# Quarter sums of the down projection's operands formed by DRAM transfers instead of DVE, in a fp32 decoder layer

## Chip, cores and metric

One core of a Trainium2 chip. The metric is the device time of one execution in microseconds (us). The kernel before ran three times; the median counts.

## What is computed

One decoder layer on a sequence of 1024 tokens with 1024 features, all in float32. Only the lines that matter here:

```
n1 = rms_norm(h, g_mix);  proj = n1 @ w_in
y_conv = short_conv_mixer(...);  y_attn = native_sparse_attention(...)
h = h + concatenate([rms_norm(y_conv), rms_norm(y_attn)]) @ w_out
u = causal_dwconv(rms_norm(h, g_ffn) @ w_up, w_ffn_conv)
u_gate, u_val = split(u)
h = h + (silu(u_gate) * u_val) @ w_down          # D_FF = 2816
h = h + sigmoid(rms_norm(h, g_ple) @ w_ple_gate) * (p @ w_ple_proj)
return rms_norm(h, g_final)
```

The attention has three branches: compressed blocks, the best 8 selected blocks of 64 keys, and a window of 512.

## The kernel before

Float32 products are formed from parts: each operand x is split into hi (a rounded copy, made on ACT, line 101) and lo = x - hi (DVE, line 104), and `mm3` (lines 189 to 193) issues three matmuls, hi by hi, hi by lo and lo by hi. The order of work on each engine is set by the framework's scheduler, from a simulated timeline, within the dependencies; the order of transfers of one queue is set with it. SP's queue issues nearly all loads and stores, POOL's queue the accumulating transfers; each queue issues in order, so one transfer that waits for a free buffer holds all behind it.

The stages are: the input projections (to about 280 us), the attention in eight blocks of 128 queries in the order 3, 7, 6, 5, 4, 2, 1, 0 (to about 550 us), the out projection `out_half` (its weights are raw tiles `out_r`, split into `out_p`), the norm that gives the operands `m` of the up phase, the up phase (22 pairs j of a gate and a value column block, to about 1075 us), the down phase (to about 1295 us), the gate of the layer embedding and the final norm.

Up and down use a scheme of seven products for a 2x2 block multiplication instead of eight. The up phase takes for pair j the raw weights `ugr` and `uvr` (`up_weights`, line 1004), forms from their halves four sums on DVE (`ut` in two parts, `u7s`, `u3s`, lines 1018 to 1021), and splits all into parts. `up(j)` (line 1149) runs the seven products; ACT copies (`e`) and DVE additions drain them from PSUM, then come the convolution of three taps (lines 1179 to 1181), silu and a multiplication (line 1184) on DVE, and the result `uc` is stored to DRAM as `ad[j]` (line 1185).

The down phase goes through the products n in the order 1, 2, 6, 5, 7, 3, 4 with 11 steps each. Its weights `down_r` are 256 KB each; the sums that products 5, 6, 7 and 3 need are formed in DRAM (`wsum`) by eight POOL transfers in the attention stage (`down_weights`, line 922, one per block at line 955). The activations come back from `ad` as `ar` (line 1199, 22 loads of 512 KB), and the sums of their halves that the seven products need are formed on DVE (lines 1204 to 1216): 55 operations. Each operand is then split on ACT and DVE into `a`, and the products accumulate in PSUM (`da`, `db`, `d`); `res_add` adds or subtracts a finished product from the residual stream `hres`.

Beside these: in the attention, `factor` (line 584) makes on POOL the factors `sf` and others, `choose` (line 644) subtracts a maximum from `sc` on POOL and normalises it (lines 649 and 660), `finish` adds the block's output `ya` on POOL (line 825); the mask copies `mk` (line 716) are on POOL too. `attn_norm` (line 900) normalises `ya` into `yan` before the second half of the out projection.

## Time and profile before

| | us |
|---|---|
| three runs | 1409.8, 1407.91, 1410.55 |
| median | 1409.8 |
| the profiled execution | 1407.71 |
| its span in the trace | 1405.8 |

The profiled execution is 2.1 us below the median, and the span lies 1.9 us below its own time (work around the span). Sums are made against the profiled execution. PE in the profile is TensorE. A busy PE may still run at the lower clock; the views by stretches give the granted clock as a share of full speed (PEclk) and the number of matmuls started.

### The profile page before, as it was taken

What the parts mean: (1) busy time and instruction counts of PE and PEld (TensorE: products, weight loads), DVE (VectorE), ACT (ScalarE), POOL (GpSimd) and SP (SyncE); (2) the same over time, 40 slices, a digit from 0 to 9 for tenths busy, and PEclk for the clock granted to TensorE, in tenths of its full rate; (3) what the DMA queues carried; (4) which work ended last, traced back from release to release, by engine and by line L of the source; (5) the groups of instructions that cost most, each with busy time, mean ns of one, the idle gap of its engine ahead of it and who ended that gap; (6) DMA issues with size and microseconds to landing.
All of it is one profiled execution on the core that took longest, in us unless ns stands there. A gap on an engine that the chain in (4) does not pass through costs nothing.

```text
span 1405.8 us, 17553 instructions
## 1 busy us (share of the span) xinstructions
PE 1349.2 (96%) x6395; PEld 1061.7 (76%) x6395; DVE 990.3 (70%) x1803; ACT 643.0 (46%) x1095; POOL 141.7 (10%) x155
## 2 busy tenths in 40 slices
PE   8989999999999988899999999999997999999995
PEld 6879888865666666687888888888885788888884
DVE  7752332478777775798976887679878985667668
ACT  6232111177767652455543444345445434546433
POOL 0211001231222444000000000000000000000001
PEclk9999999999999999899999999999999899999998
DMA  7473211132635566741222222222257833322434
GB/s 271 114 182 120 97 46 45 30 97 76 113 113 113 165 165 176 234 169 51 90 75 84 76 80 87 78 73 93 75 178 250 327 94 94 98 75 60 152 104 179
DMA packets 78933, 168.82 MB, mean 120 GB/s; under 512 B 6912, under 2 KB 28416, under 8 KB 78848
## 3 DMA queue, kind: packets, MB, share of 16 engines
q1 hardware_dynamic: 69632, 141.49, 31.3%
q0 software_dynamic: 9216, 26.22, 7.6%
q8 instruction: 50, 0.82, 0.2%
q14 instruction: 35, 0.29, 0.1%
HBM read 133.08 MB, written 51.38 MB: 131 GB/s over the span
## 4 chain that ended last, share of the span: by engine, by line
PE 88%; DVE 6%; DMA 2%; SPq 1%; issue 1%; ACT 1%; POOL 0%; DVEq 0%; ACTq 0%; POOLq 0%
PE ua L193 4%; PE ua L191 4%; PE ua L192 4%; PE uc L191 3%; PE uc L193 3%; PE uc L192 3%; PE sy L770 2%; PE da L191 2%; PE d L193 2%; PE d L191 2%; PE d L192 2%; PE da L192 2%; PE wy L770 2%; PE da L193 2%; PE g L191 2%; PE g L192 2%
## 5 line engine op out<-in xcount | busy, mean ns | idle before, releaser
L1358 POOL DMA_DIRECT2D out_dram<-h x8 | 4.4, 555 | 826.1 <-DVE h L1357 826.1
L101 ACT ACTIVATE down_p<-down_r 128x512 fp32r<-128x512 f32 x77 | 47.8, 626 | 72.8 <-PE da L193 26.1
L104 DVE TENSOR_TENSOR down_p<-down_r,down_p 128x512 fp32r<-128x512 f32 x77 | 52.4, 687 | 29.3 <-ACT down_p L101 29.2
L1179 ACT ACTIVATE uc<-xg,vec 128x1024 f32<-128x1024 f32 x22 | 25.3, 1151 | 97.0 <-DVE xg L1172 97.0
L1172 DVE TENSOR_TENSOR xg<-uc,e 128x512 f32<-128x512 f32 x22 | 15.2, 691 | 74.3 <-PE uc L193 74.1
L101 ACT ACTIVATE in_h<-in_r 128x1024 fp32r<-128x1024 f32 (+1 forms) x20 | 20.7, 1037 | 96.6 <-PE cx L192 30.1
L191 PE MATMUL da<-a,down_p 128*128 128x512 f32 x132 | 54.2, 411 | 7.7 <-ACT down_p L101 7.7
L101 ACT ACTIVATE a<-ar 128x512 fp32r<-128x512 f32 x66 | 40.5, 624 | 35.1 <-PE d L193 16.0
L104 DVE TENSOR_TENSOR a<-ar,a 128x512 fp32r<-128x512 f32 x66 | 44.5, 686 | 14.7 <-ACT a L101 14.5
L722 ACT ACTIVATE ps<-ps,stat 128x512 f32<-128x512 f32 (+7 forms) x64 | 49.1, 770 | 12.4 <-DVE stat L733 12.1
L193 PE MATMUL da<-a,down_p 128*128 128x512 f32 x132 | 51.3, 404 | 3.1 <-DVE down_p L104 3.1
L192 PE MATMUL da<-a,down_p 128*128 128x512 f32 x132 | 54.2, 410 | 0.0
L193 PE MATMUL d<-a,down_p 128*128 128x512 f32 x132 | 52.1, 395 | 0.0
L191 PE MATMUL d<-a,down_p 128*128 128x512 f32 x132 | 52.1, 395 | 0.0
L192 PE MATMUL d<-a,down_p 128*128 128x512 f32 x132 | 52.0, 394 | 0.0
L104 DVE TENSOR_TENSOR in_l<-in_r,in_h 128x1024 fp32r<-128x1024 f32 (+2 forms) x22 | 25.0, 1141 | 28.3 <-ACT in_h L101 28.2
L191 PE MATMUL g<-g,pg_h 128*128 128x256 f32 (+1 forms) x128 | 43.5, 339 | 0.0
L192 PE MATMUL g<-g,pg_h 128*128 128x256 f32 (+1 forms) x128 | 43.2, 338 | 0.0
L193 PE MATMUL g<-g,pg_l 128*128 128x256 f32 (+1 forms) x128 | 43.1, 338 | 0.0
L641 ACT ACTIVATE pw<-pw,stat 128x640 f32<-128x640 f32 (+3 forms) x56 | 38.2, 685 | 6.0 <-DVE stat L695 3.2
L101 ACT ACTIVATE ugh<-ugr 128x1024 fp32r<-128x1024 f32 x22 | 23.4, 1061 | 37.4 <-DMA ugr<-in_w_up_dram 37.1
L101 ACT ACTIVATE uth<-ut 128x1024 fp32r<-128x1024 f32 x22 | 23.3, 1061 | 37.1 <-DVE ut L1019 37.1
(789 smaller groups left out, 4457.7 us busy)
## 6 DMA issues: line engine op xcount, KB each, us to landing
wsum<-in_w_down_dram POOLq DMA_DIRECT2D x6, 2816.0 KB, 18.8
uvr<-in_w_up_dram SPq DMA_DIRECT2D x22, 512.0 KB, 3.6
ugr<-in_w_up_dram SPq DMA_DIRECT2D x22, 512.0 KB, 4.4
ad<-uc SPq DMA_DIRECT2D x22, 512.0 KB, 2.6
ar<-ad SPq DMA_DIRECT2D x22, 512.0 KB, 5.9
down_r<-wsum SPq DMA_DIRECT2D x44, 256.0 KB, 2.6
in_r<-in_w_in_dram SPq DMA_DIRECT2D x18, 512.0 KB, 6.8
down_r<-in_w_down_dram SPq DMA_DIRECT2D x33, 256.0 KB, 4.4
```

The costliest lines, as they stand in the source:

```text
L101: nc.scalar.activation(hi, x, AF.Copy)
L104: (nc.gpsimd if (lo_eng or lo_of[0]) == "pool" else nc.vector).tensor_sub(lo, x, f32(hi))
L191: first = nc.tensor.matmul(ps, wh, mh, start=start, stop=False, **more)
L192: nc.tensor.matmul(ps, wh, ml, start=False, stop=False, **more)
L193: return first, nc.tensor.matmul(ps, wl, mh, start=False, stop=stop, **more)
L641: nc.scalar.activation(w[:, :b.nw * P], w[:, :b.nw * P], AF.Exp, bias=b.M_W[:, h:h + 1], scale=-1.0, accum_out=b.D_W[:, h:h + 1])
L722: nc.scalar.activation(w[:, :nk], w[:, :nk], AF.Exp, bias=b.M_S[:, h:h + 1], scale=-1.0, accum_out=b.D_S[:, h:h + 1])
L770: m = nc.tensor.matmul(py[64 * g:64 * g + 64, :], vals(n, g), pts[g], start=n == 0, stop=n == nblk - 1)
L1172: nc.vector.tensor_add(xg[:, hi], c, e2)
L1179: nc.scalar.activation(u, xe[:, 0:S], AF.Copy, scale=col(tap))
L1358: nc.gpsimd.dma_start(out[k], o)
```

## The change

Four things.

1. The sums of the activations that the down phase needs are formed by POOL transfers from DRAM to DRAM in the up phase (`act_sums`, called after each store of `ad[j]`): for j below 11 a copy of one half to three places (768 KB), a copy of the other half (256 KB) and an accumulating transfer of 768 KB, for j from 11 two accumulating transfers (768 and 256 KB), 55 in all. The signs that an addition can't give are put into what is stored: `ad[j]` is stored with one half negated, the weights of products 1 and 7 are negated in their split, and `res_add` takes other signs.
2. `operand` loads each of the 77 operands (256 KB) straight into its page and splits it in place; no `ar`, no sums on DVE. The first four go into pages of another size (`wpage`, in the profile "fp"), and each is issued behind an earlier weight load.
3. The weight sums of four pairs of the up phase (0, 1, 20, 21) are formed in DRAM (`usum`) as well, and `up_weights` loads them for these pairs. Together with the eight transfers of `wsum` these are 24, issued four a block in six blocks, two in the middle of the block (behind `factor`'s work) and two at its end.
4. The sides of two products change: `res_sq` of half 0 moves from product 5 to product 2, `res_split` from product 3 to product 6.

```diff
+    def split(x, hi, lo, hi_eng="act", lo_eng=None, minus=False):
+        if minus:
+            nc.scalar.activation(hi, x, AF.Copy, scale=-1.0)
+            nc.vector.scalar_tensor_tensor(lo, x, -1.0, f32(hi), op0=ALU.mult, op1=ALU.subtract)
+            return
...
-                split(raw, hi, lo)
+                split(raw, hi, lo, minus=key[:5] in ("down1", "down7"))
...
-        for do, dst, src in ((copy, w5, a[1][0]), (more, w5, a[1][1]), (copy, w6, w5), (more, w6, a[0][0]),
-                             (copy, w3, w6), (more, w3, a[0][1]), (copy, w7, a[1][0]), (more, w7, a[0][0])):
-            behind(do(dst, src), pooled[0])
-            yield
+        down_ = chain([[w_down[u * (NF // 2):(u + 1) * (NF // 2)][:, :, hs(q)].rearrange("j p n -> p j n") for u in range(2)]
+                       for q in range(2)], *(wsum[q].rearrange("j p n -> p j n") for q in range(4)))
+        up_ = []
+        for r, j in enumerate((0, NF - 2)):
+            a = [[w_up[2 * j + q:2 * j + q + 3:2][:, :, hs(u)].rearrange("j p n -> p j n") for u in range(2)] for q in range(2)]
+            dst = usum[2 * r:2 * r + 2].rearrange("j p n -> p j n")
+            up_.append(chain(a, *(dst[:, :, k * 512:k * 512 + 512] for k in (1, 0, 2, 3))))
+        for items in zip(down_, *up_):
+            for do, dst, src in items:
+                behind(do(dst, src), pooled[0])
+                yield
...
         merge((selected(cur), 9, 0, 1), (values(cur), min(i + 1, 5) + 3, 0, 1), (some(fill, more[0]), more[0], 0, 1))
+        for _ in range(2):
+            next(dsums, None)
...
         merge(*gens)
-        next(dsums)
+        for _ in range(2):
+            next(dsums, None)
...
-        nc.vector.tensor_add(t[:, two], v[:, one], v[:, two])
-        nc.vector.tensor_add(t[:, one], g[:, one], t[:, two])
-        nc.vector.tensor_add(a7, g[:, one], v[:, one])
-        nc.vector.tensor_add(a3, g[:, two], t[:, one])
+        if j in SUMMED:
+            src = usum[SUMMED[j]]
+            load(t, src[:, 0:S])
+            load(a7, src[:, S:S + 512])
+            load(a3, src[:, S + 512:])
+        else:
+            nc.vector.tensor_add(t[:, two], v[:, one], v[:, two])
...
-        nc.vector.tensor_mul(us[1], us[0], us[1])
+        plus, minus = (hs(0), hs(1)) if j < NF // 2 else (hs(1), hs(0))
+        nc.vector.tensor_mul(us[1][:, plus], us[0][:, plus], us[1][:, plus])
+        nc.vector.scalar_tensor_tensor(us[1][:, minus], us[0][:, minus], -1.0, us[1][:, minus], op0=ALU.mult, op1=ALU.mult)
         load(ad[j], us[1])
+        act_sums(j)
...
+    def act_sums(j):
+        a, d = ad[j], asum[j % NH_]
+        def three(half):
+            return a[:, half].unsqueeze(1).to_broadcast([P, 3, 512])
+        if j < NH_:
+            nc.gpsimd.dma_start(d[:, 0:3], three(one))
+            nc.gpsimd.dma_start(d[:, 3], a[:, two])
+            nc.gpsimd.dma_start(d[:, 0:3], three(two), accum_op=ALU.add)
+        else:
+            nc.gpsimd.dma_start(d[:, 1:4], three(two), accum_op=ALU.add)
+            nc.gpsimd.dma_start(d[:, 2], a[:, one], accum_op=ALU.add)
...
     def operand(n, j):
-        while len(raws) < min(NF, (j if n == 1 else j + NH_ if n == 2 else NF) + 5):
-            raws.append(page([P, S], f"ar{len(raws)}"))
-            load(raws[-1], ad[len(raws) - 1])
...
+        src = {1: ad[j][:, one], 2: ad[j + NH_][:, one], 3: ad[j + NH_][:, two],
+               5: asum[j][:, 0], 6: asum[j][:, 1], 4: asum[j][:, 2], 7: asum[j][:, 3]}[n]
+        t = (wpage if n == 1 and j < 4 else page)([P, 2, 512], f"a{n}_{j}", F32R)
+        hi, lo = t[:, 0], t[:, 1]
+        x = load(f32(lo), src)
+        if len(sent_w) > 3:
+            behind(x, sent_w[-3])
+        operands[n, j] = in_place(lo, hi)
...
     def begin_down():
-        prepare(3)
+        prepare(4)
```

The number of matmuls stays (6160 rows of PE in both programs). DVE has 1738 rows instead of 1787, ACT 938 instead of 939, POOL 203 instead of 136, SP 432 instead of 365.

How the order of the instructions moves at three places:

ACT, at the start of the second half of the out projection (`facc` is the sum of squares, `an0rr` the root of the attention norm, `yan` its operands, `out_p` the split weights). Before:

```order
L221 ACTIVATE facc_5084<-hx_4122 128x512
L233 ACT_TABLE_LOAD
L233 ACTIVATE an0rr<-an0s,eps 128x16
L224 ACTIVATE f11sq<-hx_4386 128x512
L101 ACTIVATE yan_5148<-ya_2052 128x512
L101 ACTIVATE yan_5152<-ya_2053 128x512
L101 ACTIVATE yan_5156<-ya_2054 128x512
L101 ACTIVATE out_p<-out_r 128x512 x2
```

Now:

```order
L227 ACTIVATE facc_5102<-hx_4139 128x512
L105 ACTIVATE out_p<-out_r 128x512 x2
L239 ACT_TABLE_LOAD
L239 ACTIVATE an0rr<-an0s,eps 128x16
L230 ACTIVATE f11sq<-hx_4405 128x512
L105 ACTIVATE out_p<-out_r 128x512
L105 ACTIVATE yan_5166<-ya_2054 128x512
```

The two weight tiles are split ahead of the norm's root, no longer behind three of its four results; DVE's order follows.

SP's queue, at the turn from up to down, from the sixth of the `ar` loads that stand together. Before:

```order
L1199 DMA ar_8916<-ad 128x1024
L1199 DMA ar_8922<-ad 128x1024
L155 DMA down_6_r<-in_w_down_dram 128x512
L1199 DMA ar_8948<-ad 128x1024
L1199 DMA ar_8971<-ad 128x1024
L1185 DMA ad<-uc_8670 128x1024
L155 DMA down_1_r<-in_w_down_dram 128x512
```

Now, from the first weights of the down phase on:

```order
L159 DMA down_0_r<-in_w_down_dram 128x512
L159 DMA down_3_r<-in_w_down_dram 128x512
L159 DMA down_1_r<-in_w_down_dram 128x512
L1248 DMA a_4_9034<-ad 128x512
L159 DMA down_6_r<-in_w_down_dram 128x512
L1215 DMA ad<-uc_8752 128x1024
L1248 DMA a_0_8990<-ad 128x512
L1248 DMA a_1_8994<-ad 128x512
L1248 DMA a_2_8998<-ad 128x512
L159 DMA down_2_r<-in_w_down_dram 128x512
```

Three weight loads come ahead of all operands but none of the 512 KB loads is left; of the operands, a_1 (and a_3, further on) wait for matmuls that read their pages.

POOL, in the first attention block of the loop (`sf`, `sc`, `pc`, `wf` are the work of `factor` and `choose`, `ya` the output of the block). Before:

```order
L589 TENSOR_TENSOR sf_2194<-stat_1726,gates 128x4x64 x2
L649 TENSOR_TENSOR sc_2197<-sc_2197,stat_2061 128x512
L660 TENSOR_TENSOR sc_2197<-sc_2197,stat_2061 128x512
L683 TENSOR_TENSOR pc_2364<-sc_2197,gates 128x4x64 x2
L589 TENSOR_TENSOR wf_2369<-stat_2061,gates 128x4x64 x2
L825 TENSOR_TENSOR ya_2052<-ws_2186,ss_2377 128x128
```

Now:

```order
L600 TENSOR_TENSOR sf_2196<-stat_1728,gates 128x4x64 x2
L948 DMA wsum<-in_w_down_dram 128x11x512
L948 DMA usum<-in_w_up_dram 128x2x512
L660 TENSOR_TENSOR sc_2201<-sc_2201,stat_2063 128x512
L671 TENSOR_TENSOR sc_2201<-sc_2201,stat_2063 128x512
L694 TENSOR_TENSOR pc_2368<-sc_2201,gates 128x4x64 x2
```

Two transfers stand between `sf` and `sc` where there was none; the other two of a block follow the four `ya`.

## Rows read from the trace of the kernel before

**Rows 1.** The page: span, busy time by engine, and the chain's shares.

```profile
span 1405.8 us, 17553 instructions
...
PE 1349.2 (96%) x6395; PEld 1061.7 (76%) x6395; DVE 990.3 (70%) x1803; ACT 643.0 (46%) x1095; POOL 141.7 (10%) x155
...
PE 88%; DVE 6%; DMA 2%; SPq 1%; issue 1%; ACT 1%; POOL 0%; DVEq 0%; ACTq 0%; POOLq 0%
```

**Rows 2.** Stretches: us, busy of PE, PEld, DVE, ACT, POOL, PEclk, DMA share, GB/s.

```profile
555.00:600.00 45.00, 35.60 (x139) 27.23 (x138) 34.26 (x50) 18.95 (x29) 2.94 (x2) 0.89 0.77 223
655.00:665.00 10.00, 6.66 (x21) 4.69 (x20) 8.80 (x18) 3.72 (x6) 0.00 (x0) 0.83 0.00 0
1065.00:1100.00 35.00, 24.16 (x83) 18.18 (x82) 31.09 (x46) 15.57 (x23) 0.00 (x0) 0.80 0.66 222
1120.00:1155.00 35.00, 35.00 (x152) 28.31 (x151) 30.64 (x50) 14.30 (x24) 0.00 (x0) 1.00 0.40 121
700.00:1040.00 340.00, 340.00 (x1466) 274.93 (x1466) 258.66 (x345) 145.21 (x190) 0.00 (x0) 1.00 0.24 83
```

**Rows 3.** Timeline of PE: start, us, line, operation, idle before.

```profile
565.41 0.79 PE L191 MATMUL oa<-yan,out_p 128*128 128x512 f32 x1 [6.69 <-DVE yan L104]
...
659.20 0.50 PE L191 MATMUL ua<-m,uth 128*128 128x512 f32 x1 [3.31 <-ACT uth L101]
...
661.05 0.63 PE L191 MATMUL ua<-m,uth 128*128 128x512 f32 x1
```

**Rows 4.** Timeline of ACT at the start of the out projection.

```profile
562.83 2.02 ACT L101 ACTIVATE yan<-ya 128x512 fp32r<-128x512 f32 x3 [2.84 <-DVE ya L915]
564.75 1.13 ACT L101 ACTIVATE out_p<-out_r 128x512 fp32r<-128x512 f32 x2
```

**Rows 5.** Timeline of DVE at the start of the up phase.

```profile
656.64 0.69 DVE L1018 TENSOR_TENSOR ut<-uvr 128x512 f32<-128x512 f32 x1
...
658.09 0.69 DVE L1021 TENSOR_TENSOR u3s<-ugr,ut 128x512 f32<-128x512 f32 x1
```

**Rows 6.** Timeline of SP's queue at the turn.

```profile
1055.45 12.39 SPq L1199 DMA_DIRECT2D ar<-ad  x6
```

**Rows 7.** The chain of waits at the turn, in order of time.

```profile
1067.94 5.07 DMA down_r<-in_w_down_dram
```

**Rows 8.** Timeline of DVE at the turn: first and last of 16 sums.

```profile
1061.69 0.68 DVE L1212 TENSOR_TENSOR ar<-ar 128x512 f32<-128x512 f32 x1
...
1093.15 0.68 DVE L1216 TENSOR_TENSOR ar<-ar,ar 128x512 f32<-128x512 f32 x1
```

**Rows 9.** DMA issues in 312:340, 357:380, 546:552, 555:600, 700:1040: KB, us to landing.

```profile
wsum<-in_w_down_dram POOLq DMA_DIRECT2D x1, 2816.0 KB, 12.6
...
wsum<-in_w_down_dram POOLq DMA_DIRECT2D x1, 2816.0 KB, 18.3
...
wsum<-in_w_down_dram POOLq DMA_DIRECT2D x1, 2816.0 KB, 23.8
...
out_r<-in_w_out_dram SPq DMA_DIRECT2D x1, 256.0 KB, 2.5
...
out_r<-in_w_out_dram SPq DMA_DIRECT2D x5, 256.0 KB, 5.6
...
ugr<-in_w_up_dram SPq DMA_DIRECT2D x17, 512.0 KB, 4.4
```

**Rows 10.** Timeline of POOL in the attention and at its end.

```profile
372.30 1.04 POOL L649 TENSOR_TENSOR sc<-sc,stat 128x512 f32<-128x512 f32 x1 [2.18 <-DVE stat L647]
...
547.56 1.87 POOL L927 DMA_DIRECT2D wsum<-in_w_down_dram  x1
```

**Rows 11.** Timeline of ACT and PE inside the up phase.

```profile
830.25 1.06 ACT L101 ACTIVATE ugh<-ugr 128x1024 fp32r<-128x1024 f32 x1 [0.81 <-DMA ugr<-in_w_up_dram]
...
834.40 0.59 ACT L1159 ACTIVATE e<-ua 128x512 f32<-128x512 f32 x1
...
839.98 0.39 PE L191 MATMUL ua<-m,uth 128*128 128x512 f32 x1
```

More of the change, by code (lines that the diff above doesn't have):

```diff
@@ L156, in fetch @@
             raw_of[key] = raw
+            if key.startswith("down"):
+                sent_w.append(sent_load[0])
     def send(upto):
@@ L298, in hybrid_layer @@
     wsum = dram.tile([4, NF // 2, P, 512], F32, name="wsum")
+    usum = dram.tile([4, P, 2048], F32, name="usum")
+    asum = dram.tile([NF // 2, P, 4, 512], F32, name="asum")
+    SUMMED = {0: 0, 1: 1, NF - 2: 2, NF - 1: 3}
     for n in DOWN:
@@ L920, in hybrid_layer, with sums_in_dram, chain @@
     attn = {}
-    def down_weights():
-        a = [[w_down[u * (NF // 2):(u + 1) * (NF // 2)][:, :, hs(q)].rearrange("j p n -> p j n") for u in range(2)]
-             for q in range(2)]
-        w5, w6, w7, w3 = (wsum[q].rearrange("j p n -> p j n") for q in range(4))
+    def sums_in_dram():
         copy, more = nc.gpsimd.dma_start, lambda d, s_: nc.gpsimd.dma_start(d, s_, accum_op=ALU.add)
-        for do, dst, src in ((copy, w5, a[1][0]), (more, w5, a[1][1]), (copy, w6, w5), (more, w6, a[0][0]),
-                             (copy, w3, w6), (more, w3, a[0][1]), (copy, w7, a[1][0]), (more, w7, a[0][0])):
-            behind(do(dst, src), pooled[0])
-            yield
-    dsums = down_weights()
+        def chain(a, w5, w6, w7, w3):
+            return [(copy, w5, a[1][0]), (more, w5, a[1][1]), (copy, w6, w5), (more, w6, a[0][0]),
+                    (copy, w3, w6), (more, w3, a[0][1]), (copy, w7, a[1][0]), (more, w7, a[0][0])]
+        down_ = chain([[w_down[u * (NF // 2):(u + 1) * (NF // 2)][:, :, hs(q)].rearrange("j p n -> p j n") for u in range(2)]
[9 more added lines that the diff above has]
+                yield
+    dsums = sums_in_dram()
     hx, ah, al = [], [], []
@@ L1008, in up_weights @@
         v, g = (rawpage([P, S], f"u{q}r{j}") for q in "vg")
-        load(v, w_up[2 * j + 1])
+        h_ = hs(1) if j in SUMMED else slice(0, S)
+        load(v[:, h_], w_up[2 * j + 1][:, h_])
         load(g, w_up[2 * j])
@@ L1192, in hybrid_layer @@
     one, two = hs(0), hs(1)
-    raws, operands = [], {}
-    def operand(n, j):
-        while len(raws) < min(NF, (j if n == 1 else j + NH_ if n == 2 else NF) + 5):
-            raws.append(page([P, S], f"ar{len(raws)}"))
-            load(raws[-1], ad[len(raws) - 1])
-        v = nc.vector
-        b11, b12 = (raws[j][:, t] for t in (one, two))
-        b21, b22 = (raws[j + NH_][:, t] for t in (one, two)) if n != 1 else (None, None)
-        if n == 6:
-            x = page([P, 512], f"a6{j}t")
-            v.scalar_tensor_tensor(x, b11, -1.0, b22, op0=ALU.mult, op1=ALU.subtract)
-        elif n == 7:
-            v.tensor_sub(b12, b22, b12)
-        x = x if n == 6 else {1: b11, 2: b21, 5: b11, 7: b12, 3: b22, 4: b21}[n]
-        parts = operands[n, j] = halves_of(f"a{n}_{j}")
-        split(x, *parts)
-        if n == 1:
-            v.tensor_sub(b11, b11, b12)
-        elif n == 2:
-            v.tensor_sub(b21, b21, b22)
-        elif n == 5:
-            v.tensor_sub(b21, b21, b11)
+    operands = {}
+    def act_sums(j):
[9 more added lines that the diff above has]
+            nc.gpsimd.dma_start(d[:, 2], a[:, one], accum_op=ALU.add)
+    def operand(n, j):
+        src = {1: ad[j][:, one], 2: ad[j + NH_][:, one], 3: ad[j + NH_][:, two],
[6 more added lines that the diff above has]
+        operands[n, j] = in_place(lo, hi)
     steps_of = [(n, j) for n in DOWN for j in range(NH_)]
@@ L1333, in hybrid_layer @@
             add(gnorm, 1)
-            for c in range(4):
-                add(res_split, c, 0)
     tail = [(operands.pop((4, j)), weights(f"down4_{j}", ahead=2)) for j in range(NH_ - tails, NH_)]
@@ L1341, in hybrid_layer @@
             next(gsteps[1])
-        res_add(4 + c, 0, A[c])
+        res_add(4 + c, 0, A[c], -1)
         res_split(4 + c, 0)
```

23 lines of the change are left out of this document (13 added, 10 removed).

## Prediction

> **What bounds the kernel now.** I read the shares of the page first: TensorE is busy for 1349.2 of 1405.8 us, and the chain that ended last runs over TensorE for 88% of the span, over DVE for 6% and over DMA for 2% [rows 1]. The change leaves the number of matmuls as it is, so it can only give back time in which TensorE stands idle or runs at its lower clock because it stood idle. The second view, busy time by stretches, says where that is. In the up phase, 700 to 1040 us, TensorE is busy without a break and starts 1466 matmuls in 340 us, 0.232 us each; from 1120 us on it is full again [rows 2]. Three seams are not full [rows 2], and each loss is the stretch less its matmuls at 0.232 us:
> - the start of the out projection, 555 to 600 us: 139 matmuls, 45 - 32.2 = 12.8 us lost;
> - the start of the up phase, 655 to 665 us: 21 matmuls, 10 - 4.9 = 5.1 us lost;
> - the turn from up to down, 1065 to 1100 us: 83 matmuls, 35 - 19.3 = 15.7 us lost.
>
> Together 33.6 us. A few matmul records may be missing, so these are upper figures. The granted clock in these stretches is 0.89, 0.83 and 0.80 of full: after the idle gap at the up start matmuls take 0.63 us [rows 3] where 0.39 is usual in the up phase [rows 11], the lower of the two levels (1.2 GHz instead of 2.4), so part of each loss follows the gap.
>
> The third view, the timelines around each gap, gives what ends the wait. At the out projection TensorE idles 6.69 us until 565.41 [rows 3]. The profile names yan, but what the matmul also reads, out_p, is converted on ACT only at 564.75, in order behind three yan that waited 2.84 us for the normalised ya [rows 4]. At the up start TensorE idles 3.31 us until 659.20 for uth [rows 3]; DVE reached the first weight sum only at 656.64, and the last ends at 658.78 [rows 5]. At the turn, SP's queue is held for 12.39 us by six activation loads that wait for pages, and only then, at 1067.94, come the weight loads for which TensorE waits [rows 6]; the chain has that load with 5.07 us [rows 7].
>
> **The change part by part.**
>
> A, the turn. The 22 ar loads of 512 KB and the 55 sums and differences on DVE go. One of these takes 0.68 us, and 16 of them start from 1061.69 to 1093.15 us [rows 8]: 55 x 0.68 = 37.4 us of DVE in all, 16 x 0.68 = 10.9 us of them at the seam, where DVE is busy 31.09 of 35 us [rows 2] and the drains of the last up pairs queue behind these sums. In their place come 77 loads of 256 KB straight into the operand page. SP now issues the first weights before the operands, so the block of 12.39 us ahead of the weight loads goes. What is late next: a_1 and a_3 wait for fp pages that TensorE must let go, and behind them stand down_2 and down_5. So I do not take all: between 3 us (only the 5.07 us load wait shrinks, by about half) and 15 us (all), I take 10, nearer to the upper end since the late load on the chain and DVE's sums both lose their cause.
>
> B, the up start. For pair 0 (and 1, 20, 21) four DVE adds go; the sums come by three loads that are issued long before. Three of them, 656.64 to 658.78, stood right ahead of uth [rows 5]. Between 2 and 5 us back; I take 4, as the conversions of m just ahead remain.
>
> C, the out projection. The order changes: ACT and DVE convert two out_p tiles right after the first hx, ahead of the norm chain. Also the last of the weight adds, which was in flight from 547.56 for 23.8 us [rows 9, 10], now runs two blocks earlier, so the out_r loads no longer share the transfers with it: 5.6 us each beside it, 2.5 us without [rows 9]. The next tiles of out_r still need raw tiles that the first two must free. The gap of 6.69 us goes almost whole; between 2 us (the wait moves to the third out_p) and 11 us I take 7.
>
> D, attention. 24 transfers go out in six blocks, four a block, in place of one in each of eight. Two of each four now stand on POOL in mid-block between sf and sc. An add takes POOL 1.87 us to issue [rows 10]; two in front of sc make up to 3.7 us, and sc there already waited 2.18 us for DVE [rows 10], so up to 1.5 us a block remains: six blocks, 9 us at most, nothing at least, for TensorE must also run out of other work. An add that waits for its copy holds POOL too, and behind it wait the mask copies and sc: a copy lands after 12.6 us, an add after 18.3 us [rows 9], and the gap from mid-block to block end is about as long. TensorE has the out projection and the window part to do meanwhile. I take 2, between 0 and 9, near the cover.
>
> The Trainium skill ("DMA: Bandwidth & Descriptors", section "Anatomy of one DMA") fits a transfer as 2.0 us and its bytes at 436 GB/s; by that the 2816 KB would need 8.6 us as an estimate. The trace does not agree: 12.6 us for a copy, 18.3 for an add, and by the rule D would come out at 0 instead of 2.
>
> E, the up phase. Each pair adds transfers from DRAM to DRAM by POOL, otherwise idle: up to j = 10 copies of 1 MB and an add of 768 KB, then adds of 1 MB. With the rates above (12.6 us and 18.3 us for 2816 KB) that is 4.6 + 5.0 = 9.6 us per pair, of 84 x 0.232 = 19.5 us. The share of the DMA engines rises from 0.24 [rows 2] by about half, and the weight loads overlap it. ugr lands in 4.4 us today [rows 9], and ACT already waited 0.81 us for it at 830.25 [rows 11]. Beside an add, out_r took 5.6 instead of 2.5 us; times that ratio ugr would take 9.9 us, 5.5 us later. The conversion ugh stands ahead of the drain e at 834.40 on ACT, and the bank that e frees is written at 839.98 [rows 11]: e is done at about 835.0, so the cover is 5 us. At the bound of 5.5 us and with the next loads held too, I allow 1 us per pair, 22 us; at least nothing. I take 3, since an add fills only a quarter of each pair's time. The last multiplication of each pair becomes two of half the size: one more instruction on DVE per pair, at no cost, since DVE is busy for 258.66 of 340 us there [rows 2].
>
> The signs (activation scale -1 and scalar_tensor_tensor instead of a subtraction) are instructions of the same size on the same engines; cost 0, covered by the steady down phase in which TensorE waits for nothing [rows 2]. There the loads grow from 11.5 to 20.2 MB, and the DMA share of 0.40 from 1120 us on leaves room for it.
>
> **The sum.** -10 - 4 - 7 + 2 + 3 = -16 us. The profiled execution took 1407.7 us, so 1391.7; the median of the runs, 1409.8, is 2.1 us above the profiled one, so the prediction is 1394 us. With all bounds at their good end 31 us go (1379), with all at their bad end 7 are gained and 31 lost (1434).
>
> **The rivals.**
> 1. The up phase stalls on loads (slower). Where POOL's adds delay ugr by over the 5 us of cover, ACT's in-order queue keeps e from freeing the bank and TensorE waits in every pair. It decides from a landing of about 9.5 us on. For: the 5.6 against 2.5 us of out_r, and the 0.81 us that ACT waits already. Against: 700 to 1040 us shows no idle time, and the add overlaps a part of the loads only. 1 us by 22 pairs: -21 + 2 + 22, 1412.8 us; chance 0.13.
> The Trainium skill says of this (same page, section "Issuing engines are not separate DMA queues") that transfers of every issuing engine run on the same 16 DMA engines and interleave, so POOL's queue is no lane of its own. The doubled out_r landing agrees.
> 2. The turn stays. The operand loads wait for fp pages in SP's order, the weights behind them come late again, and A gives 1 us. For: a_1 and a_3 wait for TensorE, and 77 loads want more issues of SP than 22. Against: the weights for the first steps now stand ahead. 1394 + 9 = 1403 us; chance 0.14.
> 3. Almost all is given back, -29 us with D and E at zero, 1381 us. For: three seams with one cause each, all removed. Against: the queues that are late next. Chance 0.10.
> 4. Attention pays. The transfers hold POOL in each of six blocks, sc and the choice of blocks come late and TensorE runs out of work: D at 9, and in two blocks a wait for a copy that lands after 12.6 us where some 9 us lie between its issue and the add's, 7 more. 1394 + 14 = 1408 us, which is no change. For: POOL is in order. Against: TensorE is filled with other blocks' work. Chance 0.07.
>
> **How the numbers follow.** The forecast (1384 to 1402) has the rest, 0.56. 0.2% is 2.8 us, about what a measurement of this kernel can tell from no change. Faster than that come out the forecast, rival 2 and rival 3: 0.80. Within it lies rival 4: 0.07. Slower is rival 1: 0.13. The range from 1379 to 1411 takes in the good end of the bounds and rivals 2, 3 and 4; what it leaves out is rival 1 and a remainder at either end.
>
> **What would show it.** A: 1065 to 1100 us (or the same stretch, moved) starts over 120 matmuls, no ar loads, and no SP wait of over 5 us ahead of the first down weights; wrong if TensorE still waits there for a weight or an operand. B: no wait for uth at the up start. C: out_p is converted before the norm chain and the idle of 6.69 us is gone, with no add in flight. D: 300 to 490 us shows TensorE as full as before and the idle time before sc on POOL is small; wrong if the attention stage ends over 5 us later. E: the window 700 to 1040 us stays at 340 us busy and ugr lands within 9 us; if TensorE waits for ua or for uth in each pair, the prediction is wrong and rival 1 holds.

## The result, and the profile after

| | before | after |
|---|---|---|
| runs | 7 | 7 |
| median, us | 1409.54 | 1397.11 |
| lowest to highest, us | 1407.41 to 1413.4 | 1392.82 to 1403.67 |
| the profiled execution, us | 1407.71 | 1392.82 |
| its span, us | 1405.8 | 1390.9 |

The ratio is 0.9908, 95% interval 0.9885 to 0.9932: faster by 0.9%, 12.4 us at the medians. The forecast was 1394 us in a range of 1379 to 1411. Two of the seven executions of the changed kernel show a mean granted clock of 0.94 (1397.17 and 1403.67 us), the other five 0.99 (1392.82 to 1397.12 us). The profiled execution of the changed kernel is its fastest run, 4.3 us below the median; the difference of the two spans, 14.9 us, is therefore the better case of the gain. A second profiled execution of the same kernel (run e9 below) has a span of 1394.0 us and gives 11.8 us.

The busy time by stretches of the changed kernel, with the columns of [rows 2], for the three seams and the up phase and for two longer stretches:

```profile
555.00:600.00 45.00, 38.24 (x161) 29.08 (x160) 36.72 (x55) 20.84 (x32) 2.97 (x2) 1.00 0.63 199
655.00:665.00 10.00, 6.57 (x23) 5.28 (x24) 6.59 (x15) 4.17 (x6) 0.00 (x0) 0.68 0.35 130
1065.00:1100.00 35.00, 34.29 (x147) 27.56 (x148) 28.26 (x41) 21.17 (x35) 2.96 (x3) 1.00 1.07 324
700.00:1040.00 340.00, 339.71 (x1465) 274.56 (x1464) 255.24 (x354) 144.21 (x191) 40.49 (x44) 1.00 0.67 160
1040.00:1110.00 70.00, 68.57 (x295) 54.95 (x294) 54.32 (x80) 36.56 (x56) 7.59 (x7) 1.00 0.96 277
280.00:550.00 270.00, 263.02 (x1473) 173.68 (x1473) 201.02 (x639) 175.22 (x396) 110.68 (x139) 0.99 0.71 164
```

The same view of the kernel before, for the last two:

```profile
1040.00:1110.00 70.00, 59.16 (x234) 46.46 (x233) 61.21 (x90) 32.67 (x49) 0.00 (x0) 0.90 0.75 261
280.00:550.00 270.00, 263.10 (x1476) 174.37 (x1475) 199.47 (x637) 176.12 (x395) 94.04 (x123) 0.99 0.48 123
```

At the turn 147 matmuls start in 35 us where there were 83, so of the 15.7 us lost there 14.8 are back (64 matmuls at 0.232 us). The out projection starts 161 in place of 139 with the clock at 1.00 (in e9 153, at 0.96). The attention starts 1473 matmuls (1476 before) and the up phase 1465 (1466 before), so both are as full as before; in the up phase the share of the DMA engines is now 0.67 in place of 0.24. The start of the up phase did not improve: 23 matmuls in place of 21, with a granted clock of 0.68.

The same places in time, in the two traces, divide the gain. The last split of out_h on ACT, at the end of the attention, starts at 552.43 before and 553.54 after (at 552.8 to 552.9 in e2, e5 and e7 below, whose attention is the same); the first product of the up phase at 632.1 and 628.3; the product behind the gap at the up start, which needs uth, at 659.2 and 658.4; the second product of the down phase (tile d) at 1114.6 and 1099.4. In e9, the changed kernel again, these are 552.79, 629.5, 659.7 and 1102.5. So, in us against the kernel before:

| stretch | predicted | measured | e9 |
|---|---|---|---|
| D, the attention | +2 | +1.1 | +0.4 |
| C, the out projection | -7 | -4.9 | -2.9 |
| B, the up start | -4 | +3.0 | +3.1 |
| E and A, up phase and turn | +3 and -10 | -14.4 | -12.6 |
| behind the turn | 0 | +0.3 | +0.3 |
| span | -16 | -14.9 | -11.8 |

The two executions of one program differ by 2 us at C and by 1.8 us at E and A, so single terms are known to about that.

The waits of TensorE over the whole span (engine and line, waited for: us in total, times, longest), changed kernel:

```profile
PE ua L197 <- ACT uth L105: 6.3, 1, 6.3
...
PE oa L197 <- ACT out_p L105: 2.9, 2, 2.4
PE oa L199 <- DVE out_p L108: 2.3, 2, 1.7
...
PE da L197 <- ACT a L105: 1.3, 1, 1.3
```

The same view of the kernel before, at the turn:

```profile
PE da L191 <- ACT down_p L101: 7.7, 2, 4.4
PE da L193 <- DVE down_p L104: 3.1, 1, 3.1
```

The 6.7 us of the out projection [rows 3] have become waits of 2.9 and 2.3 us for later tiles of out_p. The 10.8 us that TensorE waited for down_p at the turn are gone; 1.3 us for a are left. The 3.3 us for uth [rows 3] have become 6.3 us. The timelines say why (start, us, engine, line, operation, count, and in brackets the idle time before it and what ended it). DVE, changed kernel:

```profile
652.20 0.69 DVE L108 TENSOR_TENSOR m<-hx,m 128x512 fp32r<-128x512 f32 x1 [0.70 <-ACT m L105]
658.41 1.23 DVE L108 TENSOR_TENSOR utl<-ut,uth 128x1024 fp32r<-128x1024 f32 x1 [5.52 <-ACT uth L105]
```

SP's queue, changed kernel:

```profile
592.75 0.32 SPq L1042 DMA_DIRECT2D ut<-usum  x1
...
652.92 0.32 SPq L1042 DMA_DIRECT2D ut<-usum  x1
```

What SP's queue waited for, changed kernel, 590 to 660 us:

```profile
SPq L1042 <- DVE m L108: 20.5, 1, 20.5
```

ACT, changed kernel:

```profile
657.32 1.06 ACT L105 ACTIVATE uth<-ut 128x1024 fp32r<-128x1024 f32 x1 [5.16 <-DMA ut<-usum]
```

PE, changed kernel:

```profile
658.43 0.80 PE L197 MATMUL ua<-m,uth 128*128 128x512 f32 x1 [6.27 <-ACT uth L105]
```

Pair 0's sum was loaded at 592.75. Pair 1's load goes out only at 652.92: the queue has waited 20.5 us for its page, until the split of the last operand m ended on DVE at 652.89. It lands 4.4 us later, and ACT, which had waited 5.16 us, converts uth. In the kernel before, ACT converted uth as soon as the second of DVE's sums was there:

```profile
658.09 1.06 ACT L101 ACTIVATE uth<-ut 128x1024 fp32r<-128x1024 f32 x1 [2.21 <-DVE ut L1019]
```

So only two of the three sums of [rows 5], 1.4 us from 656.64 on, stood ahead of uth; the third ran beside its conversion.

At the turn, SP's queue of the changed kernel sends three weight loads from 1040.22 us on, ahead of the operands:

```profile
1040.22 5.40 SPq L159 DMA_DIRECT2D down_r<-in_w_down_dram  x3
```

The 1.3 us that TensorE still waits for a are not for a load: the operand loads wait at most 0.6 us for TensorE from 1038 to 1070 us, and the split of a comes on ACT right behind a drain e that itself waits for TensorE. What SP's queue waited for:

```profile
SPq L1248 <- PE ua L199: 0.6, 1, 0.6
```

The timeline of ACT:

```profile
1064.38 0.60 ACT L1195 ACTIVATE e<-ua 128x512 f32<-128x512 f32 x1 [2.22 <-PE ua L199]
1064.87 1.14 ACT L105 ACTIVATE a<-a 128x512 fp32r<-128x512 f32 x2
```

### The profile page after: what moved, and what is told of

The parts are those of the page before. It is cut to its first block, busy times and chain, and to the rows that moved or that the text cites. A ratio compares the mean times of both kernels' runs of the same rounds, so it can differ in the third digit from the quotient of the medians.

```text
span 1390.9 us, 17780 instructions
## 1 busy us (share of the span) xinstructions
PE 1342.0 (96%) x6395; PEld 1056.3 (76%) x6395; DVE 949.8 (68%) x1754; ACT 640.6 (46%) x1095; POOL 209.9 (15%) x226
## 4 chain that ended last, share of the span: by engine, by line
PE 87%; DVE 6%; DMA 2%; issue 2%; SPq 1%; ACT 1%; POOL 0%; DVEq 0%; ACTq 0%; POOLq 0%
PE ua L197 4%; PE ua L198 4%; PE ua L199 4%; PE uc L197 3%; PE uc L198 3%; PE uc L199 3%; PE sy L781 2%; PE d L197 2%; PE d L199 2%; PE d L198 2%; PE da L198 2%; PE da L199 2%; PE da L197 2%; PE wy L781 2%; PE g L197 2%
## 5 line engine op out<-in xcount | busy, mean ns | idle before, releaser
L108 DVE TENSOR_TENSOR a<-a 128x512 fp32r<-128x512 f32 x77 | 51.8, 687 | 31.8 <-ACT a L105 31.7
L105 ACT ACTIVATE a<-a 128x512 fp32r<-128x512 f32 x77 | 47.5, 627 | 47.3 <-DMA a<-asum 24.6
L108 DVE TENSOR_TENSOR down_p<-down_r,down_p 128x512 fp32r<-128x512 f32 x55 | 37.2, 687 | 24.6 <-ACT down_p L105 24.5
L198 PE MATMUL da<-a,down_p 128*128 128x512 f32 x132 | 51.9, 394 | 0.0
L197 PE MATMUL da<-a,down_p 128*128 128x512 f32 x132 | 50.6, 395 | 1.3 <-ACT a L105 1.3
L105 ACT ACTIVATE down_p<-down_r 128x512 fp32r<-128x512 f32 x55 | 34.2, 627 | 37.2 <-PE d L199 14.1
L199 PE MATMUL da<-a,down_p 128*128 128x512 f32 x132 | 51.1, 393 | 0.0
L1235 POOL DMA_DIRECT2D asum<-ad x11 | 8.4, 764 | 236.7 <-DMA ad<-uc 236.7
```

The source lines that it names most:

```text
L105: nc.scalar.activation(hi, x, AF.Copy)
L108: (nc.gpsimd if (lo_eng or lo_of[0]) == "pool" else nc.vector).tensor_sub(lo, x, f32(hi))
L197: first = nc.tensor.matmul(ps, wh, mh, start=start, stop=False, **more)
L198: nc.tensor.matmul(ps, wh, ml, start=False, stop=False, **more)
L199: return first, nc.tensor.matmul(ps, wl, mh, start=False, stop=stop, **more)
L1235: nc.gpsimd.dma_start(d[:, 0:3], three(one))
```

## The experiments

All are compared with the kernel before on the same chip, as is the changed kernel with its ratio 0.9908. TensorE's line 191 to 193 of the kernel before is 197 to 199 in the changed one.

**e1, all four sums loaded in place.**

```diff
-        t = page([P, S], f"ut{j}")
...
         if j in SUMMED:
             src = usum[SUMMED[j]]
+            th_, tl_ = (wpage([P, S], f"ut{q}{j}", F32R) for q in "hl")
+            sh_, sl_ = (wpage([P, S], f"us{q}{j}", F32R) for q in "hl")
+            t, a7, a3 = f32(tl_), f32(sl_)[:, one], f32(sl_)[:, two]
             load(t, src[:, 0:S])
-            load(a7, src[:, S:S + 512])
-            load(a3, src[:, S + 512:])
+            load(f32(sl_), src[:, S:])
...
```

> The changed kernel, but for the four summed pairs the sums of the weights are loaded straight into the pages of the lo parts and split in place; no page of the full pool is asked for. Theory 1 (at the start of the up phase the sum of pair 1 is loaded late, at 652.92 us, because it waits for a page of the full pool that the operands m still hold): the load goes out some 20 us or more earlier, the wait for uth falls from 6.3 us to under 1.5, and the up phase starts 5 to 7 us earlier: span about 1384 to 1386 us. Theory 2 (the conversions on ACT and DVE ahead of uth set the start, the load is only the last name on the wait): the wait stays at 3 us or more, as the 3.3 us of the kernel before, and the gain is at most 3 us.

Median 1387.11 us, ratio 0.9849 (0.9834 to 0.9863). The wait for uth is gone, as theory 1 said. But another took its place: the sum of the norm waits 3.98 us (1.4 before), and the first up product starts at 636.7 us, 8.4 us later than in the changed kernel. ACT, in order, had a conversion of pair 1 that waited 3.12 us for its load ahead of the last square of the norm, f17sq. That wait is 2.6 of the 8.4 us; the granted clock in e1 is also lower there, 0.77 from 570 to 585 us and 0.89 from 600 to 620 us, where the changed kernel has 1.00. The timeline of ACT in e1:

```profile
592.70 1.06 ACT L105 ACTIVATE ugh<-ugr 128x1024 fp32r<-128x1024 f32 x1 [3.12 <-DMA ugr<-in_w_up_dram]
593.66 0.62 ACT L230 ACTIVATE f17sq<-hx 128x512 f32<-128x512 f32 x1
```

And of PE in e1:

```profile
598.44 0.61 PE L268 MATMUL fn1s<-fn1red,same 128*128 128x16 f32 x2 [3.98 <-DVE fn1red L263]
```

**e2, pair 1 summed on DVE again.**

```diff
-    SUMMED = {0: 0, 1: 1, NF - 2: 2, NF - 1: 3}
+    SUMMED = {0: 0, NF - 2: 2, NF - 1: 3}
```

> The changed kernel, but pair 1's sums are formed on DVE as before the change (pairs 0, 20 and 21 stay loaded). Theory 1 (the late load costs what DVE's three sums did not): the wait for uth goes from 6.3 us back to about 3.3, the span falls by about 3 us to 1388. Theory 2 (TensorE waits there for the operands m and their order): no change, within 1 us of 1391.

Median 1390.32 us, ratio 0.9869 (0.9855 to 0.9884); span 1389.1. The wait for uth is 3.3 us again, the value of the kernel before. Theory 1 holds for the wait; the span fell by 1.8 us and not by 3, since this execution reached the first up product 1.1 us later. By the two ratios e2 is 5.5 us below the changed kernel, more than the 3.0 us by which the wait fell.

**e3, no sums of the up weights.**

```diff
-    SUMMED = {0: 0, 1: 1, NF - 2: 2, NF - 1: 3}
+    SUMMED = {}
...
-        for items in zip(down_, *up_):
+        for items in zip(down_):
```

> The changed kernel without any weight sums of the up projection in DRAM: no usum transfers, all pairs' sums on DVE; the eight wsum transfers still go out in the first blocks, now two in mid-block and two at the end until they are done. If the usum part (B) is worth what was measured in the profile (a loss of about 3 us at the up start, nothing at pairs 20 and 21), the span falls to about 1388. If the sums of pairs 20 and 21 are what freed the turn, the turn loses several us there (1040 to 1110 us under 285 matmuls) and the time is 1393 or more. If the 16 usum transfers cost the attention stage (D), it ends 1 us or more earlier than in the changed kernel.

Median 1420.41 us, ratio 1.0081 (1.0065 to 1.0098): slower than the kernel before, by none of the three expectations. The loss is in the attention: 1360 matmuls from 280 to 550 us where the changed kernel has 1473, and the first product with out_p at 587.9 us instead of 559.5, 28 us later. Without the usum transfers between them, the wsum transfers follow one another on POOL's queue, and most wait there for the one before. The timeline of POOL in e3:

```profile
331.64 1.11 POOL L948 DMA_DIRECT2D wsum<-wsum  x1 [15.53 <-DMA wsum<-in_w_down_dram]
...
343.98 1.88 POOL L933 DMA_DIRECT2D wsum<-in_w_down_dram  x1 [10.82 <-DMA wsum<-wsum]
...
362.76 1.09 POOL L948 DMA_DIRECT2D wsum<-wsum  x1 [11.42 <-DMA wsum<-in_w_down_dram]
...
376.85 1.90 POOL L933 DMA_DIRECT2D wsum<-in_w_down_dram  x1 [10.11 <-DMA wsum<-wsum]
...
404.47 1.91 POOL L933 DMA_DIRECT2D wsum<-in_w_down_dram  x1 [11.39 <-DMA wsum<-in_w_down_dram]
```

The same view of the changed kernel:

```profile
314.64 1.99 POOL L933 DMA_DIRECT2D wsum<-in_w_down_dram  x1
...
359.81 1.11 POOL L948 DMA_DIRECT2D wsum<-wsum  x1
...
465.52 1.11 POOL L948 DMA_DIRECT2D wsum<-in_w_down_dram  x1
...
479.44 1.94 POOL L933 DMA_DIRECT2D wsum<-in_w_down_dram  x1 [4.86 <-DMA wsum<-in_w_down_dram]
```

The changed kernel has one such wait, of 4.86 us, in place of five of 10 to 16. While POOL waits, sc and the mask copies stand behind the transfer: sc starts at 405.60 us, 1.1 us after the last of the five goes out. TensorE has three waits there that the changed kernel does not have, of 8.5, 3.6 and 7.0 us; they end 4 to 6 us after POOL's second, fourth and fifth.

**e4, the kernel before with its weight sums earlier.**

```diff
-        next(dsums)
+        for _ in range(2 if n < 2 else 1):
+            next(dsums, None)
         cur = nxt
```

> The kernel before, with one thing moved: its eight weight sums in DRAM go out two a block in the first two blocks and then one, so the last is issued two blocks earlier. Theory for C (the last sum of 2816 KB in flight beside the loads of out_r, and the instruction order that the scheduler chose for it, made the start of the out projection late): the idle of 6.7 us there goes, and the time falls by 4 to 6 us against the kernel before. Rival (the split sums and the freed DVE of the new kernel did it): the idle stays over 4 us and the time within 2 us of the kernel before. The turn (15.7 us lost) and the up start stay as they are by both.

Median 1402.23 us, ratio 0.9948 (0.9936 to 0.996): 6.3 us come from this one move. The idle of 6.7 us is gone, and the scheduler puts two splits of out_p ahead of the norm chain, as in the changed kernel. The timeline of PE in e4 has three waits left there:

```profile
559.56 0.50 PE L191 MATMUL oa<-yan,out_p 128*128 128x512 f32 x1 [0.16 <-ACT out_p L101]
...
566.00 0.50 PE L193 MATMUL oa<-yan,out_p 128*128 128x512 f32 x1 [0.58 <-DVE out_p L104]
...
570.81 0.50 PE L193 MATMUL oa<-yan,out_p 128*128 128x512 f32 x1 [1.76 <-DVE out_p L104]
```

**e5, pair 1's sum alone loaded in place.** The edit of e1, under another condition:

```diff
+        inpl = j in (1,)
...
-        if j in SUMMED:
+        if inpl:
```

> As e1, but for pair 1 alone; pairs 0, 20 and 21 load their sums as in the changed kernel. In e1 the wait for uth was gone, but conversions that wait for loads stood on ACT ahead of the last square of the norm, and the out projection ended some 8 us later. Theory (pair 1's late page is the whole loss at the up start, pair 0 must be left as it is): both are avoided, no wait for uth over 1.5 us, the norm's sum waits under 2 us, first up product at about 628 us, span 1383 to 1386 us and below e1. Rival (e1's gain came from pairs 0, 20 and 21): span 1389 or more.

Median 1383.45 us, ratio 0.9827 (0.9813 to 0.9841): below the changed kernel and below e1, the best of all runs. Among TensorE's waits none for uth is left. The stretch from 600 to 700 us in e5:

```profile
600.00:700.00 100.00, 100.00 (x456) 81.75 (x455) 88.02 (x133) 57.01 (x95) 3.61 (x5) 1.00 0.40 127
```

And in the changed kernel:

```profile
600.00:700.00 100.00, 93.73 (x424) 76.62 (x423) 82.55 (x127) 54.55 (x90) 2.63 (x3) 0.97 0.38 119
```

These are 32 matmuls more, 7.4 us, and the spans differ by 7.3 us (1383.6 and 1390.9): the wait of 6.3 us and the lower clock behind it. The load now goes out at 604.01 us, SP's queue in e5:

```profile
604.01 0.38 SPq L1047 DMA_DIRECT2D utl<-usum  x1
```

**e6, no sums of the up weights, the others in their places.**

```diff
-    SUMMED = {0: 0, 1: 1, NF - 2: 2, NF - 1: 3}
+    SUMMED = {}
...
-            for do, dst, src in items:
-                behind(do(dst, src), pooled[0])
+            for n_, (do, dst, src) in enumerate(items):
+                if n_ == 0:
+                    behind(do(dst, src), pooled[0])
                 yield
```

> As e3 (no usum), but the eight wsum transfers keep the places that they have in the changed kernel, with nothing in the places of the 16 usum transfers. Theory for D (e3 lost 28 us in the attention because each add was issued right behind its copy and held POOL until that landed; the distance between them, which the other transfers give, makes the spread harmless): the attention ends as in the changed kernel, within 1.5 us, and no wait on POOL for a wsum landing is over 6 us. The up start waits 3.3 us for uth as before the change; the time is near e2's, 1388 to 1393. Rival (the attention stage needs something else that e3 changed): it stays over 1400. If the sums of pairs 20 and 21 matter for the turn, it shows here between 1040 and 1110 us (under 285 matmuls).

Median 1390.91 us, ratio 0.988 (0.9867 to 0.9894). The attention has 1476 matmuls, and POOL waits for a wsum landing 3.88 us at most. e6 and e3 differ only in the places of the eight transfers, so it is these that e3 lacked: the distance between a transfer and the one that reads its result, as POOL's waits say. Between 1040 and 1110 us 278 matmuls start, 17 fewer than in the changed kernel: that is what was expected if the sums of pairs 20 and 21 matter, but e12 below has them and as few, so it is no proof. TensorE waits twice there, 1.27 us for a and 1.29 us for xv, and the granted clock from 1065 to 1080 us is 0.83 instead of 1.00.

**e7, the sums on DVE back.**

```diff
+    scratch = page([P, 512], "scratch")
...
+        if n in (1, 2, 5, 6, 7):
+            nc.vector.tensor_tensor(scratch, f32(lo), f32(lo), op=ALU.max)
```

> The changed kernel with one subtraction-sized operation of 128x512 on DVE (a maximum into a scratch page) for each operand of the products 1, 2, 5, 6 and 7: DVE's 37 us of the kernel before come back, SP's loads stay as in the changed kernel. Theory DVE (the sums on DVE, 10.9 us at the turn, made the turn late): the turn loses 5 us or more again, the time rises by 4 to 8 us. Theory SP (the block of six loads that waited for pages ahead of the first weights was the cause): under 2 us, the stretch of the turn keeps over 290 matmuls from 1040 to 1110 us.

Median 1401.99 us, ratio 0.9961 (0.9948 to 0.9973); by the two ratios that is 7.5 us above the changed kernel, and its span is 9.3 us longer. Between 1040 and 1110 us 256 matmuls start in place of 295 (295 also in e9), 9.0 us. DVE's sums cost that much at the turn by themselves: SP sends the first weights at 1040.57 us, as in the changed kernel. The run also takes a page, which it does not separate.

**e8, the transfers of the up phase twice.** Every copy and add of `act_sums` is issued a second time, into an array that nothing reads (j from 11 likewise):

```diff
-            nc.gpsimd.dma_start(d[:, 0:3], three(one))
-            nc.gpsimd.dma_start(d[:, 3], a[:, two])
-            nc.gpsimd.dma_start(d[:, 0:3], three(two), accum_op=ALU.add)
+            for d in (d, asum2[j % NH_]):
+                nc.gpsimd.dma_start(d[:, 0:3], three(one))
+                nc.gpsimd.dma_start(d[:, 3], a[:, two])
+            for d in (asum[j % NH_], asum2[j % NH_]):
+                nc.gpsimd.dma_start(d[:, 0:3], three(two), accum_op=ALU.add)
```

> The changed kernel with the transfers of the up phase doubled: every copy and add of the activation sums goes out a second time into a second array in DRAM that nothing reads. Theory (the loads of the up phase have 5 us of cover; with one set of transfers none was lost): the DMA share of 0.67 goes to 0.95 or so, ugr lands in 7 to 10 us, TensorE starts to wait in the pairs, 10 to 40 us in all. Rival (the weight loads are ahead by a whole pair and do not feel it): less than 3 us lost up to 1040 us.

Median 1427.43 us, ratio 1.0143 (1.0127 to 1.0158). In the up phase 79 matmuls fewer start than in the changed kernel, 18.3 us, and ugr lands in 9.5 us; beside that the turn loses 57, with 238 matmuls instead of 295 from 1040 to 1110 us. The up phase of e8, by busy time:

```profile
700.00:1040.00 340.00, 328.50 (x1386) 262.58 (x1385) 247.67 (x345) 139.73 (x184) 75.20 (x83) 0.98 0.96 225
```

The landing of ugr there (KB, us):

```profile
ugr<-in_w_up_dram SPq DMA_DIRECT2D x17, 512.0 KB, 9.5
```

TensorE's waits in e8 from 700 to 1040 us:

```profile
PE ua L197 <- ACT e L1188: 3.7, 2, 2.1
PE ub L199 <- DVE ugl L108: 3.7, 2, 1.8
PE ub L197 <- ACT ugh L105: 3.2, 3, 1.8
PE ua L197 <- ACT e L1193: 0.7, 1, 0.7
```

The landing of ugr in the changed kernel, over the same stretch:

```profile
ugr<-in_w_up_dram SPq DMA_DIRECT2D x17, 512.0 KB, 6.9
```

TensorE waits for e and for ugh (and for ugl, which is formed from it), the operations that the prediction named for its first rival, at the landing (9.5 us) that it gave for it. These are eight waits of 11.3 us together and not one in every pair; the granted clock of 0.98 in this stretch goes with the rest of the 18.3 us. With one set, ugr lands in 6.9 us and no wait of over 0.3 us is left from 700 us to the turn.

**e9, the changed kernel again.**

> The changed kernel itself again, on the chip of the following runs, since its seven runs spread from 1392.8 to 1403.7 us, wider than those of any other kernel here. If that spread is its own, it shows again (over 6 us from lowest to highest); if it belongs to the chip of the first runs, the runs lie within 5 us, with a median of 1392 to 1396 us.

Median 1395.17 us from 1393.72 to 1398.33, ratio 0.9909 (0.9896 to 0.9922). The spread of 11 us was that of the first runs; here it is 4.6 us, and the ratio is the same. Its span, 1394.0, is 10.4 us above e5's.

**e10, the kernel before without its sums on DVE.** The 55 operations are taken out of `operand`; the products of the down phase read the loaded halves as they are.

```diff
-        if n == 6:
-            x = page([P, 512], f"a6{j}t")
-            v.scalar_tensor_tensor(x, b11, -1.0, b22, op0=ALU.mult, op1=ALU.subtract)
-        elif n == 7:
-            v.tensor_sub(b12, b22, b12)
...
-        if n == 1:
-            v.tensor_sub(b11, b11, b12)
-        elif n == 2:
-            v.tensor_sub(b21, b21, b22)
-        elif n == 5:
-            v.tensor_sub(b21, b21, b11)
```

> The kernel before without the 55 sums of activations on DVE in the down phase: the operands are the loaded halves as they stand, so the products of the down phase are left without their sums. The 22 loads of 512 KB and SP's order stay in kind. Theory DVE (the sums are the larger cause at the turn): of the 15.7 us lost there over 8 come back, 1398 to 1402 us. Theory SP (the six loads that wait for pages ahead of the first weights): under 5 us come back, 1404 us or more.

Median 1401.47 us, ratio 0.9946 (0.9932 to 0.996), 6.4 us below the kernel before on this chip. From the first up product to the second product of the down phase it takes 475.8 us (635.6 to 1111.4), the kernel before 482.5, the changed kernel 471.1, of which 3.0 are lost at the up start. So of the 14.4 us of the turn DVE's sums are 6.7. SP's part was still there: six loads stand ahead of the weights for 12.85 us, ACT waits for the load behind them, and TensorE waits for down_p. SP's queue in e10:

```profile
1059.99 12.85 SPq L1199 DMA_DIRECT2D ar<-ad  x6
1072.94 4.29 SPq L155 DMA_DIRECT2D down_r<-in_w_down_dram  x3
```

ACT in e10:

```profile
1077.44 0.63 ACT L101 ACTIVATE down_p<-down_r 128x512 fp32r<-128x512 f32 x1 [3.11 <-DMA down_r<-in_w_down_dram]
```

TensorE's wait in e10:

```profile
PE da L191 <- ACT down_p L101: 5.5, 2, 4.3
```

The gain lies between the two theories: 6.7 us against "over 8" and "under 5". The median, 1401.47 us, lies in the range that theory DVE gave.

**e11, the last add late.** In the changed kernel the last add into wsum is taken out of its place and issued at the end of the last block.

```diff
-        for items in zip(down_, *up_):
-            for do, dst, src in items:
-                behind(do(dst, src), pooled[0])
-                yield
+        flat = [item for items in zip(down_, *up_) for item in items]
+        last_ = flat.pop(21)
+        for item in flat[:21] + [None] + flat[21:] + [None] * 7 + [last_]:
+            if item:
+                behind(item[0](item[1], item[2]), pooled[0])
+            yield
```

> The changed kernel with its last sum of the down projection's weights (an add of 2816 KB) issued at the end of the last attention block, as in the kernel before; the scheduler then puts the two splits of out_p behind three splits of yan again. Theory for C: the idle of 6.7 us at 558 us comes back, the out_r loads beside the add take 5 us or more, and the time rises by 4 to 6 us against the changed kernel. Rival: under 2 us.

Median 1402.99 us, ratio 0.996 (0.9946 to 0.9973): 7.8 us above e9 on the same chip, more than expected. The idle is back, the out_r loads take 5.6 us (3.6 in the changed kernel), and the scheduler's order on ACT is that of the kernel before. The timeline of PE in e11:

```profile
566.31 0.80 PE L197 MATMUL oa<-yan,out_p 128*128 128x512 f32 x1 [6.42 <-DVE yan L108]
```

The landing of out_r there:

```profile
out_r<-in_w_out_dram SPq DMA_DIRECT2D x5, 256.0 KB, 5.6
```

**e12, the copies without the adds.** The adds of `act_sums` are left out, so the products 5, 6, 7 and 4 read one half instead of a sum or difference.

```diff
-            nc.gpsimd.dma_start(d[:, 0:3], three(two), accum_op=ALU.add)
-        else:
-            nc.gpsimd.dma_start(d[:, 1:4], three(two), accum_op=ALU.add)
-            nc.gpsimd.dma_start(d[:, 2], a[:, one], accum_op=ALU.add)
+            pass
```

> The changed kernel without the 33 accumulating transfers of the activation sums; the copies stay, so the products 5, 6, 7 and 4 read one half in place of a sum or difference. Theory (one set of transfers costs the up phase nothing, ugr at 6.9 us is inside the cover): ugr lands in about 5 us, the up phase and the total stay within 2 us of the changed kernel. Rival (the adds do cost time at the turn, where the DMA engines are 0.96 busy): the time falls by 3 us or more, between 1040 and 1130 us.

Median 1397.56 us, ratio 0.9921 (0.9908 to 0.9935), 2.4 us above e9, whose interval overlaps this one. ugr lands in 4.4 us, and the up phase has 1467 matmuls: one set of adds costs it nothing. The turn is not better but worse in this trace, 276 matmuls from 1040 to 1110 us in place of 295. TensorE waits three times, 1.2 to 1.3 us each (for e, for a and for xv), where the changed kernel waits once for that long, and the granted clock falls behind them. From 1065 to 1080 us in e12:

```profile
1065.00:1080.00 15.00, 12.47 (x46) 9.35 (x45) 14.40 (x23) 10.24 (x16) 0.00 (x0) 0.89 0.68 230
```

And in the changed kernel:

```profile
1065.00:1080.00 15.00, 14.29 (x60) 11.30 (x61) 14.37 (x21) 11.67 (x19) 2.11 (x2) 1.00 1.08 330
```

Why e and xv come later with fewer transfers stays open; e6 shows the wait for xv and the lower clock too.

## Why the prediction was right, and where it was not

The sum, -16 us, came out at -14.9 between the profiled executions and at -11.8 with e9; the measured median, 1397.1, is 3.1 us above the predicted 1394. That the sum came so close is in part luck: B came out 7.0 us worse than forecast and C 2.1 us, E and A together 7.4 us better. The seams and their causes were read from the right rows, except for one.

**A, the turn: right in kind, too small.** Forecast -10 with bounds of -3 and -15; the row for the seam and the 14.4 us of the table (12.6 in e9) put it near the upper end. Of the two causes that it named, DVE's sums are shown from both sides: e10 gets 6.7 us back without them in the kernel before, e7 loses 9.0 us at the turn with them in the changed one. The two differ, so the parts do not simply add. SP's block ahead of the weights was not undone by itself. It is the remainder, 7.7 us by e10 and 5.4 us by e7; in e10, where it is left, 5.5 us of waits for down_p remain, and the longer of them, 4.3 us, ends with the load that stood behind the six. What the prediction named as late next, the loads that wait for pages, did not come: they wait 0.6 us, and the 1.3 us that TensorE still waits are for a split on ACT. The second rival, the turn that stays, is ruled out.

**B, the up start: wrong.** The step that failed is "the sums come by three loads that are issued long before". That is so for pair 0. Pair 1's sum is loaded at 652.92, because its page is one of those that the operands m hold until DVE has split them, and then costs 4.4 us of landing where two sums cost 1.4. Not -4 but +3.0. e2 takes it back by undoing it, e5 by giving the load a page of the other pool. From the first up product to the second product of the down phase e5 takes 463.6 us, 18.9 less than the kernel before; with the 14.4 us of E and A that leaves 4.5 us for B (6.3 with the 12.6 us of e9), an estimate from these differences: about what the forecast wanted from it. The row was also misread in part: of the three sums only two stood ahead of uth. Above all the prediction looked only for what the change removed there and not for the page that its replacement asks for, though it did so for the turn.

**C, the out projection: right, 2 to 4 us too large.** -4.9 and, in e9, -2.9 against -7. The two executions of the changed kernel differ from 570 to 585 us, where the granted clock is 1.00 in the first and 0.89 in e9. e4 and e11 show the mechanism from both sides: moving the last add early in the kernel before gives 6.3 us, moving it late in the changed one costs 7.8. The order on ACT and the add in flight go together, since the scheduler chooses the order by the transfers that it simulates; no run here separates them. What is left is where the prediction put it, at the later tiles of out_p (2.9 and 2.3 us). So TensorE's waits for yan and out_p fell only from 7.9 us (6.7 and 1.2) to 5.2; the rest of the gain goes with the granted clock from 555 to 600 us, 0.89 before and 1.00 after (0.96 in e9).

**D, the attention: right in size, and the danger was real.** +1.1 (e9: +0.4) against +2. The rival "attention pays" gave 16 us; e3 made it happen, with 28 us at the end of the attention stage, and e6 took it away by distance alone. What keeps the changed kernel from it is the distance that two usum transfers make between a wsum transfer and the one that reads it.

**E, the up phase: right, the cost was nothing.** ugr went from 4.4 to 6.9 us, 2.5 us later and inside the 5 us of cover; the forecast of 3 us was too much. The first rival's mechanism is shown by e8: with twice the transfers, ugr lands in 9.5 us and TensorE waits, though not in every pair. Its threshold of about 9.5 us is not contradicted, but no run lies between 6.9 and 9.5 us.

The third rival, almost all given back, gave -29 us; the prediction's own bounds make it -31 and its middle values -21, so that figure does not follow from its terms. The range held, and it was rightly no narrower: B was off by 7 us, and E and A by as much in the other direction.

## What to carry to other kernels

When an operation is replaced by a load, ask for the page that the load needs and who holds it: the last transfer of the sums was issued 157 us ahead of the load (by 496 us), and the load still came last. Transfers that depend on one another on one in-order queue must be spaced by more than a landing, or other work of that engine waits behind them (in e3 for 10 to 16 us at a time); unrelated transfers between them did this here, and the attention ended 0.4 to 1.1 us later. Where two causes stand at one seam (an engine full of sums, a queue that waits for pages), undo each by itself: here one gave 6.7 of 14.4 us in the kernel before and cost 9.0 us in the changed one, and the other was left to the difference.

## What was not expected of the hardware

The loads of the up phase grew slower at first without a price: at a DMA share of 0.67 the loads of 512 KB took 6.9 us in place of 4.4 and no matmul was lost, at 0.96 they took 9.5 us and 79 matmuls of 1465 were. Where between the two the loss begins, no run shows.

The stalls here cost more than their length, by the granted clock behind them: taking the wait of 6.3 us away (e5) gave 7.4 us up to the second product of the down phase. The stretch of 10 us that holds its end had a granted clock of 0.68 in the changed kernel.
